# A decoder trunk's feed-forward pairs: both products of a weight chunk in a row for each operand, the third product's additions pinned ahead of weight conversions, and the down projection's first two tiles ending with their last term

## The chip, the cores and the metric

The kernel runs on one core of one Trainium2 chip. The metric is the device time of one execution in microseconds (us). Before the change it is 1483.27 us, the median of 3 runs (1482.81 to 1483.72). Lower is better.

## The reference

The program is a two-layer decoder trunk on 512 tokens of width 1024, in f32. Each layer adds a gated mixture of three token mixers and then a SwiGLU feed-forward network; the change touches only the second half of a layer:

```python
x = x + g1 * (merged @ w_out)
h2 = rmsnorm(x, norm2_w) * (1 + sc2) + sh2
x = x + g2 * ((jax.nn.silu(h2 @ w_gate) * (h2 @ w_up)) @ w_down)   # D_FF = 2816
```

## The kernel before, in words

**Data.** Activations lie transposed, 8 tiles of 128 features by 512 tokens (`x`, `norm`). Every f32 operand of a product is split into a high and a low part (`hi` by ScalarE, line 325 for weights and 510 for activations; `lo` by VectorE as the difference, lines 328 and 511). A product of two blocks is then three matmuls, hi by hi, hi by lo and lo by hi, issued by `mm3`, whose line 149 is the line of all of them. Weights stream from memory in chunks of 8 blocks of 128 by 128 into `raw` (3 buffers, loads on the SyncE queue, line 232). `split_w` turns a chunk into `whi` and `wlo` (4 buffers each). `next_w(ahead)` hands out the next chunk and starts the ones that follow, `ahead_now` = 3 unless an argument says otherwise.

**The feed-forward network.** The 22 columns of 128 hidden features are done in four parts, `PARTS` = ((3,1,1), (0,0,3), (0,0,2), (0,0,3)): so many columns along with the norm, so many single ones, so many pairs; then the down projection of the part's 6, 6, 4 and 6 columns is added to `x` (8 tiles, a residual on VectorE, line 954, for each). A layer has 9 pairs, the program 18.

**A pair** (`glu_pair`) computes gate and up of two columns for 512 tokens with 7 products in place of 8, on halves of 256 tokens. Operand z = 0 is gate, z = 1 is up. There are 14 groups of 12 matmuls of 256 columns: for each z the groups B21 (into a `pair` bank, e), B11 (into a), R1 (into c), -V (onto a), B22 (onto c), T3 (onto a) and T4 (onto a). Between groups that add onto the same bank the bank's value is read out: a after B11 (ScalarE copy, line 1063, and e added by VectorE, 1064), c after R1 (ScalarE, 1069), a after -V (ScalarE, 1072), c after B22 (VectorE addition, 1077) and a after T3 (VectorE addition, 1081). A group that adds onto a bank has to wait for the read-out before it. Before the change the groups stand in the order B21 z0, B21 z1, B11 z0, B11 z1, R1 z0, R1 z1, -V z0, -V z1, B22 z0, B22 z1, T3 z0, T3 z1, T4 z0, T4 z1.

A pair takes 7 chunks, called sub 0 to sub 6 here: subs 0 and 1 (gate and up, for B21 and B11), 2 and 3 (R1 and -V), 4 and 5 (B22 and T3), 6 (T4 of both). Subs 2 to 5 are sums of weight blocks that DMA accumulation (GpSimd queue, lines 254 and 256) and two VectorE additions (262, 263) make; those additions and the conversion of subs 0 and 1 of the next pair fall into the later part of this pair.

**What orders the work.** TensorE runs in program order. On the other engines a scheduler places instructions, but what goes through `pin` keeps its program order among the pinned ones; all weight conversions of line 328, the additions 262 and 263 and the modulation dot products (line 374, with 512 KB loads into 2 `dot` buffers, line 398) are pinned. The additions 1064, 1077 and 1081 were not. Each engine then executes its list strictly in order, so an instruction that waits holds all behind it.

**Down projection.** Tile n (of 8) takes blocks n*nk to n*nk+nk-1, with one term k for each hidden column of the part, k = 0 to nk-1 in order; the last two terms come from the last pair. Their split parts (lines 510 and 511) are made while TensorE ends the pair and begins the projection. In layer 0 the `bulk` list holds 16 dot products for layer 1's modulation, which are worked off beside the down projections of the first two parts.

Of the kernel before, what the change touches and what calls it, by code (L numbers as in the profile page):

```python
# [16 lines left out]
AF = mybir.ActivationFunctionType  # L17
# [8 lines left out]
KT = D // P  # L26
# [51 lines left out]
def hybrid_trunk(ctx, tc, xT, ws, ada, cols, pool_w, qk_w, crow, pos, con, out):  # L78
# [159 lines left out]
    class Sums:  # L238
        def __init__(self, l, m, j):
            self.l, self.m, self.j = l, m, j  # L240
# [474 lines left out]
    for l in range(L):  # L715
# [241 lines left out]
        def tail(src_of, wblk_of, part, nk, nrm, last, lead=None, halved=2):  # L957

            for n in range(KT - halved):
                if n == KT - halved - 1:  # L960
                    flush_bulk()
                o = ps_mm()
                for k in range(nk):
                    mm3(o, wblk_of(n, k), src_of(k), k == 0, k == nk - 1)
                residual(n, o, 0, S, part)
                if nrm is not None:
                    nrm.add(n, 0, S)
                if last:
                    nc.sync.dma_start(out[n * P:(n + 1) * P, :], x[n])
            for h in range(2):  # L970
                c = slice(h * BLOCK, (h + 1) * BLOCK)
                for n in range(KT - halved, KT):
                    o = ps_mm()
                    for k in range(nk):
                        mm3(o[:, :BLOCK], wblk_of(n, k), cut(src_of(k), slice(None), c), k == 0, k == nk - 1)
                    residual(n, o[:, :BLOCK], h * BLOCK, (h + 1) * BLOCK, part)
                    if nrm is not None:
                        nrm.add(n, h * BLOCK, (h + 1) * BLOCK)
                        if h == 1 and n == KT - halved:
                            lead()  # L980
                    if last:
                        nc.sync.dma_start(out[n * P:(n + 1) * P, c], x[n][:, c])

        class Blocks:
            def __init__(self, per, few=2):
                self.per, self.few, self.w = per, few, {}
# [63 lines left out]
        def glu_pair():  # L1050

            both = range(2)
            e = [ps_pair()[:, 0, :BLOCK] for _ in both]
            a, c = [None] * 2, [None] * 2
            one, two = [None] * 2, [None] * 2
            w = [next_w() for _ in both]
            for z in both:
                group(e[z], w[z], 1, "B21", True)
            for z in both:
                a[z], one[z] = ps_mm()[:, :BLOCK], tmp()  # L1060
                group(a[z], w[z], 0, "B11", True)
                C11 = one[z][:, :BLOCK]
                A.activation(C11, a[z], AF.Copy)
                V.tensor_add(C11, C11, e[z])
            w = [next_w() for _ in both]
            for z in both:
                c[z], two[z] = ps_mm()[:, :BLOCK], tmp()
                group(c[z], w[z], 0, "R1", True)
                A.activation(two[z][:, BLOCK:], c[z], AF.Copy)
            for z in both:  # L1070
                group(a[z], w[z], 1, "-V", False)
                A.activation(one[z][:, BLOCK:], a[z], AF.Copy)
            w = [next_w() for _ in both]
            for z in both:
                group(c[z], w[z], 0, "B22", False)
                C12 = one[z][:, BLOCK:]
                V.tensor_add(C12, C12, c[z])  # L1077
            for z in both:
                group(a[z], w[z], 1, "T3", False)
                m22 = two[z][:, BLOCK:]  # L1080
                V.tensor_add(m22, m22, a[z])  # L1081
            w = next_w()
            for z in both:
                group(a[z], w, z, "T4", False)

            (g1, u1), (g2, u2) = one, two
            A.activation(g1, g1, AF.Silu)
            A.activation(g2[:, BLOCK:], g2[:, BLOCK:], AF.Silu, scale=-1.0)
            A.activation(g2[:, :BLOCK], a[0], AF.Silu, scale=-1.0)
            V.tensor_mul(u1, u1, g1)  # L1090
            act.append(split_from(u1))
            V.scalar_tensor_tensor(u2[:, BLOCK:], u2[:, BLOCK:], -1.0, g2[:, BLOCK:], op0=ALU.mult, op1=ALU.mult)
            V.scalar_tensor_tensor(u2[:, :BLOCK], a[1], -1.0, g2[:, :BLOCK], op0=ALU.mult, op1=ALU.mult)
            act.append(split_from(u2))

        for part, (along, single, pairs) in enumerate(PARTS):
# [28 lines left out]
            if part == 0 and l + 1 < L:  # L1125
                bulk.extend(ada_tasks(l + 1, (SC1, SH1)))
            bulk_rate[0] = 1.5
            blk = Blocks(nk, 4)
            if part + 1 < len(PARTS):
                for n in range(KT):  # L1130
                    if n == KT // 2:
                        bulk_rate[0] = 0.0
                    o = ps_mm()
                    for k in range(nk):
                        mm3(o, blk(n, k), act[k], k == 0, k == nk - 1)
                    residual(n, o, 0, S, G2)
            elif l + 1 == L:
                tail(lambda k: act[k], blk, G2, nk, None, True)
            else:
                flush_bulk()  # L1140
                drain()
                n1 = Norm()
                table(AF.Abs_reciprocal_sqrt, f32(act[-1][1])[:, 0:1])
                scratch = ps_pair()
                bank = scratch[:, 1]
                tail(lambda k: act[k], blk, G2, nk, n1, False, lead(n1, l + 1, 0, bank), 4)
                norm = n1


# [98 lines left out]
```

## Time and profile before

| | before |
|---|---|
| median of 3 runs (range) | 1483.27 us (1482.81 to 1483.72) |
| profiled execution, span from first to last instruction | 1484.8 us |
| TensorE busy | 1460.9 us, 98% |
| VectorE busy | 1050.8 us, 71% |
| ScalarE busy | 662.0 us, 45% |
| GpSimd busy | 106.9 us, 7% |
| mean granted TensorE clock | 0.999 |
| from memory | 213.65 MB read, 145 GB/s over the span |

The profiled execution has no other time of its own than its span, which is 1.5 us above the median of the timed runs. A busy matmul in this profile is counted from its start to its modelled end, and ends overlap the next starts, so a stall is read best from the distance between the starts of two matmuls: back to back they start 0.12 us apart with 256 columns and 0.227 us apart with 512 columns.

### The profile page before, as it was taken

How to read it: one execution, taken by the hardware profiler on the slowest of the kernel's cores; microseconds unless marked ns; L12 is line 12 of the kernel's file. 1: busy time of each engine (PE TensorE's matmuls, PEld its weight loads, DVE VectorE, ACT ScalarE, POOL GpSimd, SP SyncE). 2: the span in 40 equal slices, each digit the busy share in tenths (PEclk: the TensorE clock that was granted, in tenths of full speed). 3: DMA queues.
4: the chain of work that ended last, by engine and by line, in shares of the span. 5: the costliest groups of instructions: out<-in, count | busy, mean ns of one | idle time of the engine just before them, and what ended most of it. 6: DMA issues, size and time to landing. Idle time of an engine off the chain costs nothing. (4 is left out here: it accounts for less than half of the span.)

```text
span 1484.8 us, 21967 instructions
## 1 busy us (share of the span) xinstructions
PE 1460.9 (98%) x8443; PEld 1269.0 (85%) x8443; DVE 1050.8 (71%) x1855; ACT 662.0 (45%) x1138; POOL 106.9 (7%) x157
## 2 busy tenths in 40 slices
PE   9999999999999999999999999999999999999999
PEld 7888787888988998989988877778889889989997
DVE  7877888758786866657576877776587756657673
ACT  4634555443553452535444345555335524434350
POOL 0000000020000220210000000001000102211100
PEclk9999999999999999999999999999999999999999
DMA  9624344475247675734323443334552445736432
GB/s 351 206 75 169 127 142 131 139 199 175 84 131 219 196 185 189 185 100 128 107 93 125 167 162 119 110 114 138 135 185 77 127 134 146 188 97 182 135 95 84
DMA packets 84408, 217.18 MB, mean 146 GB/s; under 512 B 10832, under 2 KB 23760, under 8 KB 84304
## 3 DMA queue, kind: packets, MB, share of 16 engines
q1 hardware_dynamic: 67456, 177.37, 35.5%
q0 software_dynamic: 16128, 37.76, 11.4%
q8 instruction: 66, 1.08, 0.3%
q10 hardware_dynamic: 720, 0.66, 0.1%
q14 instruction: 38, 0.31, 0.1%
HBM read 213.65 MB, written 2.10 MB: 145 GB/s over the span
## 5 line engine op out<-in xcount | busy, mean ns | idle before, releaser
L149 PE MATMUL mm<-big,whi 128*128 128x512 f32 (+1 forms) x4362 | 1086.1, 340 | 10.3 <-DVE tmp L1081 5.9
L149 PEld LDWEIGHTS mm<-big,whi 128*128 128x128 f32 x4362 | 746.3, 190 | 101.9 <-DVE tmp L1081 9.5
L149 PE MATMUL mm<-big,wlo 128*128 128x512 f32 (+1 forms) x2181 | 737.7, 338 | 0.3 <-DVE wlo L328 0.3
L149 PEld LDWEIGHTS mm<-big,wlo 128*128 128x128 f32 x2181 | 414.4, 190 | 45.4 <-DVE wlo L328 0.8
L325 ACT ACTIVATE whi<-raw 128x1024 fp32r<-128x1024 f32 (+2 forms) x240 | 248.7, 1037 | 323.2 <-PE mm L149 277.4
L328 DVE TENSOR_TENSOR wlo<-raw,whi 128x1024 fp32r<-128x1024 f32 (+2 forms) x240 | 285.5, 1195 | 94.8 <-ACT whi L325 94.2
L325 ACT ACTIVATE whi<-w 128x1024 fp32r<-128x1024 f32 x72 | 76.4, 1061 | 131.9 <-PE mm L149 75.8
L254 POOL DMA_DIRECT2D w<-in_ws x72 | 47.0, 681 | 1007.5 <-DVE wlo L328 732.4
L954 DVE SCALAR_TENSOR_TENSOR x<-mm,mod,x 128x512 f32<-128x512 f32 (+1 forms) x90 | 62.0, 690 | 78.7 <-PE mm L149 78.7
L374 DVE SCALAR_TENSOR_TENSOR dot<-dot,csil 128x1024 f32<-128x1024 f32 x80 | 97.2, 1222 | 22.9 <-DMA dot<-in_ada 22.6
L328 DVE TENSOR_TENSOR wlo<-w,whi 128x1024 fp32r<-128x1024 f32 x72 | 87.4, 1221 | 36.5 <-ACT whi L325 36.5
L149 PE MATMUL pair<-whi,big 128*128 128x512 f32 x224 | 76.8, 390 | 0.0
L256 POOL DMA_DIRECT2D w<-in_ws x72 | 64.1, 945 | 143.7 <-DMA w<-in_ws 132.6
L149 PE MATMUL pair<-big,whi 128*128 128x256 f32 (+1 forms) x376 | 74.1, 295 | 0.0
L149 PEld LDWEIGHTS pair<-big,whi 128*128 128x128 f32 x376 | 60.5, 191 | 2.2
L149 PE MATMUL mm<-whi,big 128*128 128x512 f32 x160 | 57.2, 394 | 1.5 <-ACT big L497 1.2
L149 PE MATMUL pair<-big,wlo 128*128 128x256 f32 (+1 forms) x188 | 55.5, 295 | 1.1 <-DVE wlo L328 1.1
L511 DVE TENSOR_TENSOR big<-tmp,big 128x512 fp32r<-128x512 f32 x48 | 32.9, 692 | 29.9 <-ACT big L510 28.9
L914 DVE SCALAR_TENSOR_TENSOR big<-big,mm 128x512 f32<-128x512 f32 x48 | 32.8, 685 | 23.8 <-PE mm L149 23.4
L149 PEld LDWEIGHTS pair<-whi,big 128*128 128x128 f32 x224 | 42.1, 188 | 8.7
L149 PE MATMUL pair<-wlo,big 128*128 128x512 f32 x112 | 43.7, 390 | 0.0
L630 ACT ACTIVATE w<-mm 128x512 fp32r<-128x512 f32 (+2 forms) x48 | 24.0, 525 | 33.4 <-PE mm L155 33.2
(187 smaller groups left out, 1249.8 us busy)
## 6 DMA issues: line engine op xcount, KB each, us to landing
raw<-in_ws SPq DMA_DIRECT2D x146, 512.0 KB, 3.3
dot<-in_ada SPq DMA_DIRECT2D x80, 512.0 KB, 4.1
w<-in_ws POOLq DMA_DIRECT2D x144, 256.0 KB, 4.4
raw<-in_ws SPq DMA_DIRECT2D x64, 256.0 KB, 3.7
raw<-in_ws SPq DMA_DIRECT2D x24, 384.0 KB, 3.3
w<-in_ada SPq DMA_DIRECT2D x16, 512.0 KB, 5.7
raw<-in_ws SPq DMA_DIRECT2D x16, 448.0 KB, 4.9
raw<-in_ws SPq DMA_DIRECT2D x36, 128.0 KB, 3.2
```

The source lines that it names most:

```text
L149: tc.keep_in_program_order(T.matmul(*a, **k))
L254: nc.gpsimd.dma_start(dst, self.source(0, 1))
L256: nc.gpsimd.dma_start(dst, self.source(*other), accum_op=ALU.add)
L325: A.activation(hi[:, :n], raw[:, :n], AF.Copy)
L328: ins = V.tensor_sub(lo[:, :n], raw[:, :n], f32(hi)[:, :n])
L374: return V.scalar_tensor_tensor(aw, aw, 1.0, csil, op0=ALU.mult, op1=ALU.mult, accum_out=mod[l][:, part, j:j + 1])
L511: V.tensor_sub(lo, src, f32(hi))
L630: A.activation(both[:, :, :, 0], tp, AF.Copy)
L914: V.scalar_tensor_tensor(sg, sg, 1.0, branch, op0=ALU.add, op1=ALU.mult)
L954: V.scalar_tensor_tensor(x[k][:, lo:hi], src, mod[l][:, part, k:k + 1], x[k][:, lo:hi], op0=ALU.mult, op1=ALU.add)
```

## The change

In `glu_pair` both products of a chunk follow each other for one operand, so the groups now stand in the order B21 z0, B11 z0, B21 z1, B11 z1, R1 z0, -V z0, R1 z1, -V z1, B22 z0, T3 z0, B22 z1, T3 z1, T4 z0, T4 z1, and each chunk is asked for just ahead of its own products. The three VectorE additions (now lines 1081, 1094 and 1096) are pinned. SiLU and product of the first column (now lines 1099 and 1100) stand ahead of the T4 groups in program order. In every down projection of the feed-forward network, tiles 0 and 1 are opened together (`open_tiles`, `late` = 1): all terms but the last of tile 0, all but the last of tile 1, then the last of each; chunks first used by these two tiles are asked for with `next_w(2)` rather than 3. The number of instructions on each engine is the same as before.

```diff
+        def open_tiles(src_of, wblk_of, nk, late):
+            os = [ps_mm(), ps_mm()]
+            for ks in (range(nk - late), range(nk - late, nk)):
+                for n, o in enumerate(os):
+                    for k in ks:
+                        mm3(o, wblk_of(n, k), src_of(k), k == 0, k == nk - 1)
+            return os
+
+        def whole_tiles(src_of, wblk_of, nk, late, count):
+            ready = open_tiles(src_of, wblk_of, nk, late) if late else []
+            for n in range(count):
+                if n < len(ready):
+                    o = ready[n]
+                else:
+                    o = ps_mm()
+                    for k in range(nk):
+                        mm3(o, wblk_of(n, k), src_of(k), k == 0, k == nk - 1)
+                yield n, o
...
-                    self.w[c] = next_w(2 if n >= KT - self.few else None)
+                    self.w[c] = next_w(2 if n >= KT - self.few or n < self.early else None)
...
-            e = [ps_pair()[:, 0, :BLOCK] for _ in both]
-            a, c = [None] * 2, [None] * 2
-            one, two = [None] * 2, [None] * 2
-            w = [next_w() for _ in both]
-            for z in both:
-                group(e[z], w[z], 1, "B21", True)
+            a, c, one, two = [], [], [], []
             for z in both:
-                a[z], one[z] = ps_mm()[:, :BLOCK], tmp()
-                group(a[z], w[z], 0, "B11", True)
+                w = next_w()
+                e = ps_pair()[:, 0, :BLOCK]
+                group(e, w, 1, "B21", True)
+                a.append(ps_mm()[:, :BLOCK])
+                group(a[z], w, 0, "B11", True)
+                one.append(tmp())
                 C11 = one[z][:, :BLOCK]
                 A.activation(C11, a[z], AF.Copy)
-                V.tensor_add(C11, C11, e[z])
-            w = [next_w() for _ in both]
+                pin(V.tensor_add(C11, C11, e))
...
-            w = [next_w() for _ in both]
-            for z in both:
-                group(c[z], w[z], 0, "B22", False)
-                C12 = one[z][:, BLOCK:]
-                V.tensor_add(C12, C12, c[z])
-            for z in both:
-                group(a[z], w[z], 1, "T3", False)
-                m22 = two[z][:, BLOCK:]
-                V.tensor_add(m22, m22, a[z])
+            for z in both:
+                w = next_w()
+                group(c[z], w, 0, "B22", False)
+                C12, C22 = one[z][:, BLOCK:], two[z][:, BLOCK:]
+                pin(V.tensor_add(C12, C12, c[z]))
+                group(a[z], w, 1, "T3", False)
+                pin(V.tensor_add(C22, C22, a[z]))
             w = next_w()
+            (g1, u1), (g2, u2) = one, two
+            A.activation(g1, g1, AF.Silu)
+            V.tensor_mul(u1, u1, g1)
+            act.append(split_from(u1))
...
-            blk = Blocks(nk, 4)
+            blk = Blocks(nk, 4, 2)
...
-                tail(lambda k: act[k], blk, G2, nk, None, True)
+                tail(lambda k: act[k], blk, G2, nk, None, True, late=1)
```

Three places show what moved. The first is VectorE's list in the second half of the first pair of layer 1's second part: `w4` are the weight sums, `wlo` the converted chunks, and `mm` is bank a or c. Before:

```order
L262 TENSOR_TENSOR w42151_11788<-w42151_11788,raw2172_11931 128x512
L263 TENSOR_TENSOR w42152_11789<-w42151_11788,raw2172_11931 128x512
L328 TENSOR_TENSOR wlo2174_11937<-raw2172_11931,whi2173_11935 128x1024
L262 TENSOR_TENSOR w42153_11794<-w42153_11794,raw2175_11939 128x512
L1077 TENSOR_TENSOR tmp2160_11833<-tmp2160_11833,mm2168_11875 128x256
L263 TENSOR_TENSOR w42154_11795<-w42153_11794,raw2175_11939 128x512
L1077 TENSOR_TENSOR tmp2162_11849<-tmp2162_11849,mm2170_11890 128x256
L1081 TENSOR_TENSOR tmp2169_11876<-tmp2169_11876,mm2159_11832 128x256
L1090 TENSOR_TENSOR tmp2162_11849<-tmp2162_11849,tmp2160_11833 128x512
L328 TENSOR_TENSOR wlo2177_11945<-raw2175_11939,whi2176_11943 128x1024
L1081 TENSOR_TENSOR tmp2171_11891<-tmp2171_11891,mm2161_11848 128x256
L328 TENSOR_TENSOR wlo2179_12001<-w42151_11788,whi2178_11999 128x1024
```

And now, at the same place, where 1094 is the addition after B22, 1096 the one after T3 and 1100 the product that was line 1090:

```order
L262 TENSOR_TENSOR w42149_11786<-w42149_11786,raw2172_11931 128x512
L263 TENSOR_TENSOR w42150_11787<-w42149_11786,raw2172_11931 128x512
L328 TENSOR_TENSOR wlo2174_11937<-raw2172_11931,whi2173_11935 128x1024
L1094 TENSOR_TENSOR tmp2157_11828<-tmp2157_11828,mm2165_11868 128x256
L1096 TENSOR_TENSOR tmp2166_11869<-tmp2166_11869,mm2156_11815 128x256
L262 TENSOR_TENSOR w42151_11792<-w42151_11792,raw2175_11965 128x512
L263 TENSOR_TENSOR w42152_11793<-w42151_11792,raw2175_11965 128x512
L328 TENSOR_TENSOR wlo2177_11971<-raw2175_11965,whi2176_11969 128x1024
L1094 TENSOR_TENSOR tmp2162_11861<-tmp2162_11861,mm2170_11903 128x256
L1096 TENSOR_TENSOR tmp2171_11904<-tmp2171_11904,mm2161_11848 128x256
L1100 TENSOR_TENSOR tmp2162_11861<-tmp2162_11861,tmp2157_11828 128x512
L328 TENSOR_TENSOR wlo2179_12001<-w42149_11786,whi2178_11999 128x1024
```

The second addition after T3 has moved from behind both the product (1090) and the conversion of sub 1 to ahead of the product; the conversion of sub 1 stands ahead of it in both lists.

The second place is VectorE's list at layer 0's first down projection, whose `dot` rows are the modulation products. Before, from the conversion of the projection's chunk 3 on (the chunks count from 0):

```order
L328 TENSOR_TENSOR wlo881_4448<-raw879_4441,whi880_4446 128x1024
L374 SCALAR_TENSOR_TENSOR dot882_4456,mod1_118<-dot882_4456,csil_89 128x1024
L374 SCALAR_TENSOR_TENSOR dot883_4459,mod1_118<-dot883_4459,csil_89 128x1024
L954 SCALAR_TENSOR_TENSOR x0_77<-mm878_4440,mod0_117,x0_77 128x512
L328 TENSOR_TENSOR wlo890_4496<-raw888_4491,whi889_4494 128x1024
L954 SCALAR_TENSOR_TENSOR x1_78<-mm887_4484,mod0_117,x1_78 128x512
L374 SCALAR_TENSOR_TENSOR dot884_4462,mod1_118<-dot884_4462,csil_89 128x1024
L374 SCALAR_TENSOR_TENSOR dot885_4465,mod1_118<-dot885_4465,csil_89 128x1024
```

And now, after two products (of `dot880` and `dot881`) and a third (`dot882`) that stand ahead of these rows:

```order
L954 SCALAR_TENSOR_TENSOR x0_77<-mm878_4440,mod0_117,x0_77 128x512
L374 SCALAR_TENSOR_TENSOR dot883_4457,mod1_118<-dot883_4457,csil_89 128x1024
L954 SCALAR_TENSOR_TENSOR x1_78<-mm879_4441,mod0_117,x1_78 128x512
L374 SCALAR_TENSOR_TENSOR dot884_4472,mod1_118<-dot884_4472,csil_89 128x1024
L328 TENSOR_TENSOR wlo887_4485<-raw885_4478,whi886_4483 128x1024
L374 SCALAR_TENSOR_TENSOR dot888_4496,mod1_118<-dot888_4496,csil_89 128x1024
L954 SCALAR_TENSOR_TENSOR x2_79<-mm889_4507,mod0_117,x2_79 128x512
L374 SCALAR_TENSOR_TENSOR dot890_4514,mod1_118<-dot890_4514,csil_89 128x1024
L954 SCALAR_TENSOR_TENSOR x3_80<-mm899_4553,mod0_117,x3_80 128x512
L374 SCALAR_TENSOR_TENSOR dot891_4517,mod1_118<-dot891_4517,csil_89 128x1024
L328 TENSOR_TENSOR wlo894_4531<-raw892_4526,whi893_4529 128x1024
L328 TENSOR_TENSOR wlo897_4539<-raw895_4533,whi896_4537 128x1024
```

The conversion of chunk 3 (`wlo887`) has moved from ahead of all dot products to behind five of them, that of chunk 4 (`wlo894`) from behind two to behind eight; on the SyncE queue five dot loads now stand ahead of the load of the next pair's sub 0.

The third place is TensorE's list where tile 0 of a down projection (`mm2255`) reaches its last two terms, in layer 1's second part. `big2251` and `big2253` are the last pair's two activations before the change, `big2180` is the first term's. Before:

```order
L149 MATMUL mm2255_12558<-big2251_12548,wlo2240_12436 128x512
L149 MATMUL mm2255_12558<-big2253_12554,whi2239_12434 128x512
L149 MATMUL mm2255_12558<-big2254_12555,whi2239_12434 128x512
L149 MATMUL mm2255_12558<-big2253_12554,wlo2240_12436 128x512
L149 MATMUL mm2259_12586<-big2180_12031,whi2239_12434 128x512
```

And now, where tile 1 is `mm2256` and five terms of it (15 matmuls) stand between the first row and the last four, of which the end is shown:

```order
L149 MATMUL mm2256_12559<-big2251_12522,wlo2243_12470 128x512
L149 MATMUL mm2255_12558<-big2253_12554,whi2239_12434 128x512
L149 MATMUL mm2255_12558<-big2254_12555,whi2239_12434 128x512
L149 MATMUL mm2255_12558<-big2253_12554,wlo2240_12436 128x512
L149 MATMUL mm2256_12559<-big2253_12554,whi2242_12468 128x512
```

The last term of tile 0 has moved behind the five other terms of tile 1.

More of the change, by code (lines that the diff above doesn't have):

```diff
@@ L955, in residual, with tail @@
                                    op0=ALU.mult, op1=ALU.add)
-        def tail(src_of, wblk_of, part, nk, nrm, last, lead=None, halved=2):
-            for n in range(KT - halved):
+        def open_tiles(src_of, wblk_of, nk, late):
[15 more added lines that the diff above has]
+                yield n, o
+        def tail(src_of, wblk_of, part, nk, nrm, last, lead=None, halved=2, late=0):
+            for n, o in whole_tiles(src_of, wblk_of, nk, late, KT - halved):
                 if n == KT - halved - 1:
                     flush_bulk()
-                o = ps_mm()
-                for k in range(nk):
-                    mm3(o, wblk_of(n, k), src_of(k), k == 0, k == nk - 1)
                 residual(n, o, 0, S, part)
@@ L984, in hybrid_trunk, with __init__ @@
         class Blocks:
-            def __init__(self, per, few=2):
-                self.per, self.few, self.w = per, few, {}
+            def __init__(self, per, few=2, early=0):
+                self.per, self.few, self.early, self.w = per, few, early, {}
             def __call__(self, n, k):
@@ L1062, in glu_pair @@
                 C11 = one[z][:, :BLOCK]
                 A.activation(C11, a[z], AF.Copy)
-                V.tensor_add(C11, C11, e[z])
-            w = [next_w() for _ in both]
+                pin(V.tensor_add(C11, C11, e))
             for z in both:
-                c[z], two[z] = ps_mm()[:, :BLOCK], tmp()
-                group(c[z], w[z], 0, "R1", True)
+                w = next_w()
+                c.append(ps_mm()[:, :BLOCK])
+                two.append(tmp())
+                group(c[z], w, 0, "R1", True)
@@ L1069, in glu_pair @@
                 A.activation(two[z][:, BLOCK:], c[z], AF.Copy)
+                group(a[z], w, 1, "-V", False)
+                A.activation(one[z][:, BLOCK:], a[z], AF.Copy)
             for z in both:
-                group(a[z], w[z], 1, "-V", False)
-                A.activation(one[z][:, BLOCK:], a[z], AF.Copy)
-            w = [next_w() for _ in both]
-            for z in both:
-                group(c[z], w[z], 0, "B22", False)
-                C12 = one[z][:, BLOCK:]
-                V.tensor_add(C12, C12, c[z])
@@ L1083, in glu_pair @@
+            (g1, u1), (g2, u2) = one, two
+            A.activation(g1, g1, AF.Silu)
+            V.tensor_mul(u1, u1, g1)
+            act.append(split_from(u1))
+            A.activation(g2[:, BLOCK:], g2[:, BLOCK:], AF.Silu, scale=-1.0)
+            V.scalar_tensor_tensor(u2[:, BLOCK:], u2[:, BLOCK:], -1.0, g2[:, BLOCK:], op0=ALU.mult, op1=ALU.mult)
             for z in both:
                 group(a[z], w, z, "T4", False)
-            (g1, u1), (g2, u2) = one, two
-            A.activation(g1, g1, AF.Silu)
@@ L1127, in hybrid_trunk @@
             bulk_rate[0] = 1.5
-            blk = Blocks(nk, 4)
+            blk = Blocks(nk, 4, 2)
             if part + 1 < len(PARTS):
-                for n in range(KT):
-                    if n == KT // 2:
+                for n, o in whole_tiles(lambda k: act[k], blk, nk, 1, KT):
+                    if n == KT // 2 - 1:
                         bulk_rate[0] = 0.0
-                    o = ps_mm()
-                    for k in range(nk):
-                        mm3(o, blk(n, k), act[k], k == 0, k == nk - 1)
                     residual(n, o, 0, S, G2)
             elif l + 1 == L:
-                tail(lambda k: act[k], blk, G2, nk, None, True)
+                tail(lambda k: act[k], blk, G2, nk, None, True, late=1)
             else:
```

7 lines of the change are left out of this document (2 added, 5 removed).

## The prediction

> **What bounds the kernel now.** I read the page's first part, then who waited for whom on TensorE's weight loads, then the timeline at those waits. The page says that TensorE is the bound:
>
> ```profile
> span 1484.8 us, 21967 instructions
> PE 1460.9 (98%) x8443; PEld 1269.0 (85%) x8443; DVE 1050.8 (71%) x1855; ACT 662.0 (45%) x1138; POOL 106.9 (7%) x157
> ```
>
> So only TensorE's own waits can be won; work taken off VectorE by itself is worth nothing. The waits of its weight loads name the ones that the change touches (total us, times, longest):
>
> ```profile
> PEld mm L149 <- DVE tmp L1081: 9.5, 18, 0.6
> PEld mm L149 <- DVE big L511: 2.5, 6, 0.5
> PEld mm L149 <- ACT big L510: 2.1, 2, 1.7
> PEld pair L149 <- DVE wlo L328: 1.3, 1, 1.3
> ```
>
> There are 18 pairs, and the first row has 18 waits: one in each pair, for the addition after T3. The next two wait for the last pair's activation, the fourth for a converted weight chunk ahead of a pair. The timeline of TensorE in the first pair of layer 1's second part (start, duration, idle time before and its releaser) shows which group waits:
>
> ```profile
> 1227.07 0.40 PE L149 MATMUL pair<-big,whi 128*128 128x256 f32 x2
> ...
> 1245.67 0.28 PE L149 MATMUL mm<-big,wlo 128*128 128x256 f32 x1
> 1246.33 0.50 PE L149 MATMUL mm<-big,whi 128*128 128x256 f32 x2 [0.38 <-DVE tmp L1081]
> ...
> 1247.86 0.40 PE L149 MATMUL pair<-big,whi 128*128 128x256 f32 x2
> ```
>
> A pair is 14 groups of 12 matmuls of 0.12 us, 1.44 us a group and 20.16 us in all, but 1247.86 - 1227.07 = 20.79 us pass. The row at 1246.33 stands 12 matmuls ahead of the pair's end, so T4 of z = 1 waits, not T4 of z = 0. It should have started at 1245.79, lost 0.54, and its first two matmuls take 0.50 together where two take 0.40 in the row at 1247.86: 0.64 us in all. VectorE in the same stretch says why:
>
> ```profile
> 1242.86 0.69 DVE L263 TENSOR_TENSOR w<-w,raw 128x512 f32<-128x512 f32 x1
> 1243.46 0.42 DVE L1077 TENSOR_TENSOR tmp<-tmp,mm 128x256 f32<-128x256 f32 x1
> 1243.79 0.42 DVE L1081 TENSOR_TENSOR tmp<-tmp,mm 128x256 f32<-128x256 f32 x1
> 1244.12 0.69 DVE L1090 TENSOR_TENSOR tmp<-tmp,tmp 128x512 f32<-128x512 f32 x1
> 1244.72 1.22 DVE L328 TENSOR_TENSOR wlo<-raw,whi 128x1024 fp32r<-128x1024 f32 x1
> 1245.86 0.42 DVE L1081 TENSOR_TENSOR tmp<-tmp,mm 128x256 f32<-128x256 f32 x1
> ```
>
> T3 of z = 1 ended at 1227.07 + 12 x 1.44 = 1244.35; its addition came at 1245.86, behind a product (1090) and a conversion. VectorE has no idle time in these rows: it is late, not waiting. In the last pair of a part the loss is smaller:
>
> ```profile
> 1268.66 0.40 PE L149 MATMUL pair<-big,whi 128*128 128x256 f32 x2
> ...
> 1289.35 0.40 PE L149 MATMUL mm<-big,whi 128*128 128x512 f32 x1
> ```
>
> 1289.35 - 1268.66 = 20.69, 0.53 us over 20.16.
>
> **The change part by part: the pairs.** 10 pairs have another behind them, 8 are the last of a part: 10 x 0.64 + 8 x 0.53 = 10.6 us to win, if T4 of z = 1 no longer waits. The group row bounds it from above: 9.5 us of idle weight loads and 18 x 0.10 of restart, 11.3. What is late next? I lay the new order on the same clock, with the pair's start as zero. Lags and ScalarE's conversion are in these rows:
>
> ```profile
> 1234.46 0.38 ACT L1069 ACTIVATE tmp<-mm 128x256 f32<-128x256 f32 x1 [0.23 <-PE mm L149]
> 1237.22 1.06 ACT L325 ACTIVATE whi<-raw 128x1024 fp32r<-128x1024 f32 x1 [0.94 <-PE mm L149]
> ```
>
> R1 of z = 0 ended at 7.20 (1234.27), and its reader started 0.19 later; -V of z = 0 ended at 10.08 (1237.15), and the conversion that its weight buffer released started 0.07 later. In the new order T3 of z = 0 ends at 14.40, so its addition starts at 14.59 at the earliest. Behind it VectorE has 262 and 263, the conversion of sub 1, the addition after B22 and the one after T3 of z = 1. By the distances of the quoted rows that is 0.33 + 2 x 0.60 + 1.14 + 0.33, so the last addition starts at 17.59 (T3 of z = 1 is ready at 17.28 + 0.19) and ends at 18.01. T4 of z = 1 is due at 13 x 1.44 = 18.72: 0.7 us to spare. The conversion needs its high part: the buffer is free at 14.47, a SiLU shorter than a conversion stands ahead, so it is done by 14.47 + 2 x 1.06 = 16.6 at the latest where VectorE arrives at 16.1; that takes at most 0.5 of the 0.7. T4 of z = 0 gains a group of distance and had not waited. The other read-outs keep three groups (4.3 us) between write and next use. Weight buffers get freer: a chunk is used for two groups in a row, not over five. The pinned additions now wait ahead of conversions: behind them stands sub 1's, ready at about 17.3 and needed at 20.16 + 2.88 = 23.0. GpSimd's list has one accumulation begun earlier; SyncE's order within pairs is as before. I take 10.5 us.
>
> **The down projections.** In layer 0's third part ScalarE and TensorE show the wait for the last activation, and the windows the granted clock behind it (column PEclk, 0.50 and 0.65):
>
> ```profile
> 630.87 1.06 ACT L325 ACTIVATE whi<-raw 128x1024 fp32r<-128x1024 f32 x1 [2.68 <-DMA raw<-in_ws]
> 631.84 0.61 ACT L510 ACTIVATE big<-tmp 128x512 fp32r<-128x512 f32 x1
> 630.79 0.39 PE L149 MATMUL mm<-big,wlo 128*128 128x512 f32 x1
> 632.50 0.51 PE L149 MATMUL mm<-big,whi 128*128 128x512 f32 x1 [1.32 <-ACT big L510]
> 633.23 0.51 PE L149 MATMUL mm<-big,whi 128*128 128x512 f32 x1 [0.22 <-DVE big L511]
> 634.00:636.00 2.00, 2.00 (x6) 1.54 (x5) 0.97 (x2) 0.00 (x0) 0.00 (x0) 0.50 0.25 84
> 636.00:638.00 2.00, 2.00 (x7) 1.56 (x7) 0.00 (x0) 0.00 (x0) 0.00 (x0) 0.65 0.48 178
> ```
>
> The split of the last activation stood behind a chunk's conversion that waited for its load. TensorE lost 632.50 - 630.79 - 0.227 = 1.48 and 633.23 - 632.50 - 0.227 = 0.50, 1.98 us, where the weight loads' waits count 1.7 + 0.5 = 2.2, so a matmul loses 0.9 of what its weight load waits. Of the group rows' 2.5 + 2.1 = 4.6 us I expect 0.8 to 0.9: 3.7. The last term of tile 0 now comes nk - 1 terms later, each 3 x 0.227 = 0.68: 2.0 us later with nk = 4, 3.4 with nk = 6. That covers every one of these waits but, just, the largest: its high part came 1.48 late, its low part 633.23 - 632.50 later still, and the start comes half a us earlier. I leave 0.3 (0 to 1.0 over the two parts with four columns).
>
> The half clock cost (2 x 0.50 + 2 x 0.35) = 1.7 us. The timed runs have a median 1.5 us below the profile's span, so they may not have it; I count half, 0.9. [...]
>
> **The dot products in layer 0.** This is where the change may cost. Rows of VectorE and TensorE at the first down projection and behind it:
>
> ```profile
> 458.05 0.63 PE L149 MATMUL mm<-big,whi 128*128 128x512 f32 x2
> 460.92 0.69 DVE L511 TENSOR_TENSOR big<-tmp,big 128x512 fp32r<-128x512 f32 x1 [2.17 <-ACT big L510]
> 468.36 1.23 DVE L374 SCALAR_TENSOR_TENSOR dot<-dot,csil 128x1024 f32<-128x1024 f32 x1 [0.86 <-DMA dot<-in_ada]
> 474.12 1.22 DVE L374 SCALAR_TENSOR_TENSOR dot<-dot,csil 128x1024 f32<-128x1024 f32 x1 [1.94 <-DMA dot<-in_ada]
> 475.82 1.23 DVE L374 SCALAR_TENSOR_TENSOR dot<-dot,csil 128x1024 f32<-128x1024 f32 x1 [0.47 <-DMA dot<-in_ada]
> 478.63 1.23 DVE L374 SCALAR_TENSOR_TENSOR dot<-dot,csil 128x1024 f32<-128x1024 f32 x1 [0.92 <-DMA dot<-in_ada]
> 481.39 1.23 DVE L374 SCALAR_TENSOR_TENSOR dot<-dot,csil 128x1024 f32<-128x1024 f32 x1 [1.52 <-DMA dot<-in_ada]
> 493.79 0.39 PE L149 MATMUL pair<-big,wlo 128*128 128x256 f32 x1 [1.14 <-DVE wlo L328]
> dot<-in_ada SPq DMA_DIRECT2D x80, 512.0 KB, 4.1
> ```
>
> With two buffers a dot product follows the one two before it by a load and a product: 474.12 - 468.36 = 5.76, 478.63 - 474.12 = 4.51 and 481.39 - 475.82 = 5.57 us, mean 5.28. Chunk 4's conversion now stands behind eight products, two loaded long before. The first starts 3.5 us after the projection's start D (460.92 + 0.6 against 458.05), the second 1.15 later, the eighth three turns after the second: 4.65 + 3 x 5.28 = 20.5; product and conversion add 2.3: ready at D + 22.8. Chunk 4 starts with block 32 and its low part is used 0.45 later: 32 x 0.68 + 0.45 = D + 22.2. So TensorE waits 0.6 us (0 at turns of 4.5, 2.1 at 5.8). Chunk 3, behind five products, is ready at 4.65 + 5.28 + 2.3 + 1.2 = 13.4 plus residuals, due at 16.8. The second part has fewer products ahead: no wait. [...]
>
> The wait at 493.79 goes: it lost 1.3 and 0.1 since sub 1 was needed one group into the pair and now two. 1.4 won; if the queue of dots runs late instead, 0.
>
> **Sum.** 10.5 + 3.7 + 0.9 + 1.4 - 0.3 - 0.6 = 15.6 us. From the median 1483.27 that is 1467.7 us; the span would go from 1484.8 to 1469.2, or 1468.4 with all of the half clock gone.
>
> **The rivals.** (a) The dot queue costs more: turns of 5.8 us, 2.1 us of wait, and behind it another 3.4 us at half clock, 1.7; with 493.79 not won: 1467.7 + 1.5 + 1.7 + 1.4 = 1472.3. For it: the idle times before the products, all by DMA. Against: the two next-pair loads now come later. (b) The additions are in order, but VectorE arrives over 0.7 us late and T4 waits as before, because 262 waits for accumulations: 1467.7 + 10.5 = 1478.2. Against: VectorE has no idle time before 263 in the rows. (c) The change doesn't do what it says: every wait goes over to the next releaser; 1483. Against: the 0.7 us worked out. (d) Slower: the pinned additions hold conversions. If the sums of sub 1 land so late that 262 starts 2.3 us behind its place, 0.7 to spare and then 1.6 us a pair, the ten pairs with another behind lose 16 us, as much as the sum above gains; at 3.0 us late in each it is 1467.7 + 10 x (3.0 - 0.7) = 1490.7. Against: the same rows, and that the accumulations are begun no later.
>
> **How the numbers follow.** Forecast 0.76, (a) 0.12, (b) 0.06, (c) 0.03, (d) 0.03. The range's lower end: 11.3 + 4.6 + 1.7 + 1.4 = 19 us at the very most, of which I allow 18.3: 1465.0. The upper end holds (a) with its unknowns, 1473.5. It leaves out (b), (c) and (d), 0.12, and some of the edges. About 0.2% (3 us) is what a measurement can tell from no change: faster in the forecast, (a) and (b), 0.94; same (c), 0.03; slower (d), 0.03.
>
> **What would show it.** Right: no wait of T4 on line 1096, pairs of 20.16 us, no wait for lines 510 or 511 at a projection's start, at most one wait of 0 to 2 us for a conversion near 22 us into layer 0's first projection. Wrong: 18 waits that only name another line, VectorE idle ahead of 262, or half-clock windows in layer 0.

## The result and the profile after

The kernel after takes 1470.59 us (median of 4 runs, 1469.69 to 1471.74), the kernel before 1483.49 (4 runs, 1482.81 to 1484.62): ratio 0.9914, interval 0.9900 to 0.9928, so 12.9 us won. The forecast was 1467.7 with a range of 1465.0 to 1473.5: the sign and the range held, the gain was 2.7 us too large. Two executions of the study, one of the kernel before (5098 us) and one of e7 (2386 us), took far longer than all others and are in none of the medians below.

The page's first part, beside the one of before:

```profile
span 1467.9 us, 21907 instructions
PE 1452.6 (99%) x8443; PEld 1266.3 (86%) x8443; DVE 1050.9 (72%) x1855; ACT 664.4 (45%) x1138; POOL 106.9 (7%) x157
```

VectorE does as much as before, and TensorE is busy 8.3 us less: matmuls that restart behind a wait or run at half clock are counted longer (0.50 and 0.63 us against 0.40 in rows below). The waits of TensorE's weight loads for lines 328 and 511 that are left (total us, times, longest; of the first row only the longest, 0.7, lies in the feed-forward network):

```profile
PEld mm L149 <- DVE wlo L328: 1.0, 3, 0.7
PEld mm L149 <- DVE big L511: 0.3, 1, 0.3
```

The row with 18 waits for the addition after T3 is gone, and no other took its place: line 1096 stands in no row. The timeline of TensorE in the first pair of layer 1's second part, the same pair as in the prediction:

```profile
1215.56 0.40 PE L149 MATMUL pair<-big,whi 128*128 128x256 f32 x2
...
1234.27 0.40 PE L149 MATMUL mm<-big,whi 128*128 128x256 f32 x2
...
1235.71 0.28 PE L149 MATMUL pair<-big,whi 128*128 128x256 f32 x1
```

1235.71 - 1215.56 is 20.15 us, 14 groups at full pace, and T4 of z = 1 starts at 18.71 into the pair without a wait. VectorE in that pair:

```profile
1232.95 0.42 DVE L1094 TENSOR_TENSOR tmp<-tmp,mm 128x256 f32<-128x256 f32 x1
1233.29 0.41 DVE L1096 TENSOR_TENSOR tmp<-tmp,mm 128x256 f32<-128x256 f32 x1
1233.62 0.69 DVE L1100 TENSOR_TENSOR tmp<-tmp,tmp 128x512 f32<-128x512 f32 x1
1234.22 1.22 DVE L328 TENSOR_TENSOR wlo<-w,whi 128x1024 fp32r<-128x1024 f32 x1
```

The last addition starts 17.73 us into the pair and ends at 18.14 (forecast 17.59 and 18.01), with product and conversion behind it. 0.58 us are to spare, where 0.7 were forecast.

One wait is left in layer 0's first down projection, at the place that the prediction names:

```profile
479.82 0.50 PE L149 MATMUL mm<-big,wlo 128*128 128x512 f32 x1 [0.23 <-DVE wlo L328]
```

By the starts it lost 0.39 us and 0.11 at the next matmul, 0.5 against 0.6 forecast. Over the whole program the distances between TensorE's starts exceed full pace by some 17 us more in the profile of before than here; in the feed-forward parts alone they exceed it by 17.4 us there and 0.7 here. So the traces say 17 us and the clock says 12.9. That difference is what the first experiment is about.

### The profile page after: what moved, and what is told of

The parts are those of the page before. It is cut to its first block, busy times and chain, and to the rows that moved or that the text cites. A ratio compares the mean times of both kernels' runs of the same rounds, so it can differ in the third digit from the quotient of the medians.

```text
span 1467.9 us, 21907 instructions
## 1 busy us (share of the span) xinstructions
PE 1452.6 (99%) x8443; PEld 1266.3 (86%) x8443; DVE 1050.9 (72%) x1855; ACT 664.4 (45%) x1138; POOL 106.9 (7%) x157
## 3 DMA queue, kind: packets, MB, share of 16 engines
q0 software_dynamic: 16128, 37.76, 11.9%
## 4 chain that ended last, share of the span: by engine, by line
PE 88%; DVE 7%; DMA 2%; ACT 2%; issue 1%; SPq 0%; DVEq 0%; ACTq 0%
PE mm L149 75%; PE pair L149 11%; PE mm L155 2%; DMA dot<-in_ada 2%; DVE wlo L328 1%; DVE dot L374 1%; ACT whi L325 1%; DMA w<-in_ada 0%; ACT tmp L612 0%; ACT tmp L614 0%; DMA x<-in_xT 0%; DVE tmp L619 0%; DVE w L374 0%; DVE big L514 0%; DVE big L914 0%
## 5 line engine op out<-in xcount | busy, mean ns | idle before, releaser
L1081 DVE TENSOR_TENSOR tmp<-tmp,pair 128x256 f32<-128x256 f32 x36 | 15.2, 422 | 40.1 <-ACT tmp L1080 40.1
```

The costliest lines, as they stand in the source:

```text
L1081: pin(V.tensor_add(C11, C11, e))
```

## The experiments

**e1: the kernel before, once more.** No edit.

> The kernel before, unchanged, to see how much of its profiled execution's stalls belong to every execution. Theory A (my sum, as it stands): the wait of 1.98 us around 632.50 and the 1.7 us at half clock behind it are in about half of all executions; the new profile's span is 1483 to 1485 us, and a stretch with PEclk about 0.5 may be there. Theory B (the one profile was a slow one): time minus span is 1.8 us in the kernel after, so timed runs of 1483.3 us have spans of about 1481.6, 3 us under the profile's 1484.8; the new profile shows about 1481.6, no half clock between 634 and 638 us, and a wait under 0.5 us at the third part's down projection. The 18 waits of T4 (10.6 us with their restarts) stand in both.

Measured: 1483.68 us (11 runs), 1483.06 for its comparison runs (21), ratio 1.0006 (0.9997 to 1.0015). The profiled execution has a span of 1480.7 us, 4.1 less than the first profile. Its waits:

```profile
PEld mm L149 <- DVE tmp L1081: 9.6, 18, 0.6
PEld mm L149 <- DVE big L511: 1.4, 4, 0.5
PEld mm L149 <- DVE wlo L328: 0.9, 1, 0.9
PEld mm L149 <- ACT big L510: 0.5, 2, 0.3
```

And TensorE at the third part's down projection, where the first profile had lost 1.98 us and then 1.6 at half clock:

```profile
630.25 0.49 PE L149 MATMUL mm<-big,whi 128*128 128x512 f32 x1
630.97 0.50 PE L149 MATMUL mm<-big,whi 128*128 128x512 f32 x1 [0.23 <-DVE big L511]
631.32 0.40 PE L149 MATMUL mm<-big,wlo 128*128 128x512 f32 x1
```

Here 0.6 are lost and the clock stays up. The wait for a chunk ahead of a pair (1.4 at 493.79) isn't there either; the 0.9 for line 328 lies outside the feed-forward network. The 18 waits of T4 are the same to 0.1 us. Theory B holds: the pairs' loss belongs to every execution, the others differ from one to the next. They end with a load. ScalarE's conversion ahead of the last split, whose row of the first profile (630.87) the prediction shows, waits for its load here too, but less:

```profile
628.62 1.06 ACT L325 ACTIVATE whi<-raw 128x1024 fp32r<-128x1024 f32 x1 [1.85 <-DMA raw<-in_ws]
```

Counted from the late start of T4 in the pair before it (626.61 here, 627.41 there) it starts 2.0 us on and not 3.5. At 493.79 it is the load of a dot product: that product waited 0.78 us for it at 487.11 in the first profile, and not at all here. In the runs that list both, the time is the span plus 1.8 us. The first profile's execution therefore took about 1486.6 us, as long as the longest of the 61 timed runs of this kernel in the study (1480.9 to 1486.5, median 1483.1).

**e2 and e3: the two halves of the change.** e2 has the new `glu_pair` and the down projections as before; against the kernel after it is

```diff
-            blk = Blocks(nk, 4, 2)
+            blk = Blocks(nk, 4)
...
-                for n, o in whole_tiles(lambda k: act[k], blk, nk, 1, KT):
+                for n in range(KT):
...
+                    o = ps_mm()
+                    for k in range(nk):
+                        mm3(o, blk(n, k), act[k], k == 0, k == nk - 1)
```

e3 has the down projections of after and the `glu_pair` of before, without pins; its diff against after is that of the function in the section on the change, the other way round.

> Only the new order of the pairs (with its pins); the down projections open their tiles one after the other as before. My sum: 10.5 us for 18 waits of T4 and 1.4 for the wait at 493.79, so 1483.5 - 11.9 = 1471.6 us, and the waits for lines 510 and 511 at the projections' starts (3.6 us of TensorE in before) still there in the profile. Rival (the profile overstated the pairs too, by the ratio of the measured 12.9 us to the 15.6 predicted): 1483.5 - 9.8 = 1473.7. Rival (the pairs' wins come only together with the down edit): under 8 us won.

> Only the down projections' new start (late 1, early 2); the pairs as before. My sum: 3.7 - 0.3 - 0.6 = 2.8 us, and 0.9 of half clock, so 1480.7 down to 1479.8 us, and the 18 waits of T4 still there. Theory B (the big wait and the half clock are seldom in a timed run): 3.7 less 1.98 less 0.6 of dot products is 1.1 us won, 1482.4. Rival (the dot products ahead of chunk 4 eat it): 1483.5 or slower.

Measured: e2 1473.20 us (5 runs), ratio 0.9939 (0.9927 to 0.9951), 9.9 us won where I expected 11.9. e3 1481.19 (11 runs), ratio 0.9988 (0.9980 to 0.9997), 1.9 won, between the sum and theory B. Together 11.8, between the 12.9 that the whole change won here and the 10.9 that it won beside e11 below: within what such comparisons differ by, the halves add up. They are not independent, though, as e2's waits show:

```profile
PEld mm L149 <- DVE big L511: 3.4, 6, 0.8
PEld mm L149 <- ACT big L510: 3.1, 3, 1.0
```

6.5 us of waits at the projections' starts, against 1.9 in e1 and 4.6 in the first profile of before: pairs that no longer wait reach the projection before the last activation is split. The stalls of T4 had been hiding a part of the starts' wait. In e2's profiled execution (its slowest, 1476.75 us) the half clock came as well:

```profile
628.27 0.50 PE L149 MATMUL mm<-big,whi 128*128 128x512 f32 x1 [0.42 <-DVE big L511]
...
629.60 0.50 PE L149 MATMUL mm<-big,whi 128*128 128x512 f32 x1 [0.60 <-ACT big L510]
630.33 0.63 PE L149 MATMUL mm<-big,whi 128*128 128x512 f32 x1 [0.22 <-DVE big L511]
630.76 0.63 PE L149 MATMUL mm<-big,wlo 128*128 128x512 f32 x1
```

Three gaps of 0.58, 0.77 and 0.50 us, none as long as the 1.48 of the first profile of before, and from 630.33 on matmuls start 0.427 us apart instead of 0.227.

**e4: only the pins,** in before's order of groups:

```diff
-                V.tensor_add(C11, C11, e[z])
+                pin(V.tensor_add(C11, C11, e[z]))
-                V.tensor_add(C12, C12, c[z])
+                pin(V.tensor_add(C12, C12, c[z]))
-                V.tensor_add(m22, m22, a[z])
+                pin(V.tensor_add(m22, m22, a[z]))
```

> Before's order of groups, with its three additions pinned and nothing else: VectorE then does both additions after T3 ahead of the product and of one conversion. My theory (the group order makes the room): T3 of z = 0 ends at 15.84 us into the pair and T4 of z = 0 is due at 17.28, 1.44 later, and a conversion of 1.2 us and the additions after B22 stand ahead of its addition, so T4 waits still, now for z = 0 as well: 0 to 4 us won, 1480 to 1483.5. Rival (the pins do all of it, the group order nothing): all 18 waits go, 10.5 us won, 1473.0. Rival (pins hold conversions): slower than before by 2 us or more, with waits for converted chunks in the pairs.

Measured: 1521.92 us (5 runs), ratio 1.0252 (1.0236 to 1.0268), 38.9 us slower. Neither my 0 to 4 won nor the rival's 10.5: T4 now waits much longer, and for z = 0.

```profile
PEld mm L149 <- DVE tmp L1081: 36.9, 18, 2.1
```

ScalarE, VectorE and TensorE in one pair:

```profile
1262.99 1.06 ACT L325 ACTIVATE whi<-raw 128x1024 fp32r<-128x1024 f32 x1 [2.99 <-PE mm L149]
1264.08 1.22 DVE L328 TENSOR_TENSOR wlo<-raw,whi 128x1024 fp32r<-128x1024 f32 x1 [0.74 <-ACT whi L325]
1265.22 0.74 DVE L1077 TENSOR_TENSOR tmp<-tmp,mm 128x256 f32<-128x256 f32 x2
1265.88 0.75 DVE L1081 TENSOR_TENSOR tmp<-tmp,mm 128x256 f32<-128x256 f32 x2
1266.35 0.51 PE L149 MATMUL mm<-big,whi 128*128 128x256 f32 x2 [1.84 <-DVE tmp L1081]
```

All four additions run together, in order, and all late: a conversion now stands ahead of them whose high part waits for a buffer, and that buffer comes free when T3 of z = 0 ends. T4 of z = 0 was due at 1264.35 and starts at 1266.35. The rival that pins hold conversions had the sign, with the parts exchanged: a conversion holds the additions. In the change itself the pins do nothing: the program built without them, and with SiLU and product behind T4 again, has its instructions in the same order on all five engines, row for row; it was not run. So the order of the groups, with the requests for chunks that go with it, is all there is to the pairs' gain.

**e9 and e10: which groups.** e9 changes only the third row (B22, T3, B22, T3) of before's `glu_pair`, e10 only the first two, in the same way for B21 with B11 and for R1 with -V; neither has pins. e9 against before:

```diff
-            w = [next_w() for _ in both]
             for z in both:
-                group(c[z], w[z], 0, "B22", False)
+                w = next_w()
+                group(c[z], w, 0, "B22", False)
...
-            for z in both:
-                group(a[z], w[z], 1, "T3", False)
+                group(a[z], w, 1, "T3", False)
```

> The kernel before with one thing of the change: B22 z0, T3 z0, B22 z1, T3 z1 in that order, each chunk asked for ahead of its own two groups; no pins, the first eight groups and the down projections as before. In the ten pairs with another behind them VectorE then has, behind the addition after B22 of z = 1, one 263 and one conversion ahead of the last addition. My theory (only the place of the last addition matters): it starts 15.84 + 0.19 + 0.33 + 0.60 + 1.14 = 18.1 us into the pair and ends at 18.5, T4 of z = 1 is due at 18.72, so nothing waits, with 0.2 to spare: as the pairs-only kernel, 1473 us. Rival (the conversion's high part comes late, since its buffer is free only when T3 of z = 0 ends): up to 0.5 us in each of ten pairs, 1473 to 1478. Rival (the first eight groups' order is needed too): the 18 waits stay, 1483.

> The other part of the pairs' change alone: B21 z0, B11 z0, B21 z1, B11 z1, R1 z0, -V z0, R1 z1, -V z1, each chunk asked for ahead of its own groups; B22, T3 and everything else as before, no pins. My theory: the last addition still stands behind a product and a conversion, so the 18 waits on the addition after T3 stay: 1483 us, within 1.5. Rival (buffers that come free sooner let VectorE run ahead, and that was the gain): 1473 us.

Measured on one chip: e9 1476.04 us (6 runs), ratio 0.9952 (0.9937 to 0.9967); e10 1475.61 (5 runs), ratio 0.9953 (0.9941 to 0.9965). e9 went as expected in the pairs: no wait for an addition is left, although the last one has only some 0.1 us to spare. In the pair that began at 1220.14 it ends 18.60 us in:

```profile
1238.33 0.41 DVE L1080 TENSOR_TENSOR tmp<-tmp,mm 128x256 f32<-128x256 f32 x1
```

Its time is 3 us over the 1473 that I expected, and its six runs lie far apart (1472.5 to 1479.3). What it lacks stands at the starts, 4.4 us of waits for line 511 and 4.1 for 510. e10 went against my theory, which gave it nothing:

```profile
PEld mm L149 <- DVE tmp L1079: 3.8, 8, 0.5
```

8 of the 18 waits are left, those of the pairs that are the last of a part; the ten others are gone. A timeline of VectorE in one of the ten, which began at 1218.49:

```profile
1228.29 1.23 DVE L328 TENSOR_TENSOR wlo<-raw,whi 128x1024 fp32r<-128x1024 f32 x1 [1.05 <-ACT whi L325]
...
1234.37 0.69 DVE L1088 TENSOR_TENSOR tmp<-tmp,tmp 128x512 f32<-128x512 f32 x1
1234.98 0.41 DVE L1079 TENSOR_TENSOR tmp<-tmp,mm 128x256 f32<-128x256 f32 x1
1235.54 1.23 DVE L328 TENSOR_TENSOR wlo<-raw,whi 128x1024 fp32r<-128x1024 f32 x1 [0.15 <-ACT whi L325]
1236.68 0.41 DVE L1079 TENSOR_TENSOR tmp<-tmp,mm 128x256 f32<-128x256 f32 x1
```

The last addition is still behind a conversion, as I had said, but it ends at 18.60, not at 19.2: chunks used for two groups in a row free their buffers sooner. ScalarE's conversion ahead of the first row starts 8.71 us into the pair, just behind the end of -V of z = 0 at 8.64 (10.15 and 10.08 in the same pair of before). The conversion in the first row then starts at 9.80 (11.24 in before), and the last addition comes 0.6 us earlier. So either row alone is enough for the ten pairs, by two different ways, and the third row is needed for the eight.

**e5: how much is to spare, and when the clock drops.** Extra additions ahead of the last one, in another number for each pair:

```diff
+EXTRA = ((1, 1, 2, 3, 4, 6, 7, 8, 9), (2, 7, 8, 9, 10, 2, 12, 8, 3))
...
+                for _ in range(EXTRA[l][pairs_done[0]] if z else 0):
+                    pin(V.tensor_add(two[1][:, :BLOCK], one[1][:, :BLOCK], one[1][:, :BLOCK]))
                 pin(V.tensor_add(C22, C22, a[z]))
+            pairs_done[0] += 1
```

> The kernel after, with n extra additions of 256 columns on VectorE (0.33 us each) ahead of the addition after T3 of z = 1; n is 1, 1, 2, 3, 4, 6, 7, 8, 9 for the nine pairs of layer 0 and 2, 7, 8, 9, 10, 2, 12, 8, 3 for those of layer 1. The extra sums go to a buffer that is overwritten later; the output is the same. My theory: in the trace of after that addition ends 18.14 us into a pair and T4 of z = 1 is due at 18.72, so 0.58 us are to spare and T4 waits 0.33 n - 0.58: nothing for 1, 0.1 for 2, 0.4 for 3, 2.06 for 8, 3.4 for 12; over the ladder 24 us and 1.5 of restarts. Rival: that addition is not what is next in line (a conversion or a SiLU is), and the first step that costs is another. On the clock: theory G (a fixed grid of windows of 3.41 us, half clock for one window when more than about 1.9 us of the window before was idle) gives stretches of 3.4 us at half clock, 1.5 us lost in each, behind some of the gaps of 2.06 us and more and behind none of the shorter ones: about 1503 us in all. [...]

Measured: 1515.4 us (one run). T4 waits in 14 pairs, for that addition and nothing else:

```profile
PEld mm L150 <- DVE tmp L1101: 33.9, 14, 4.9
```

By the starts, the pairs with another behind them lose 0.28 us with 2 extras, 1.19 with 4, 2.58 with 7, 3.04 with 8, 3.95 with 10 and 4.88 with 12: 0.46 n - 0.64. An extra addition cost 0.46 (six take 2.72 us together), not the 0.33 that I took from additions into different buffers, which makes 9 of the 12 us by which the total is over my figure; two starts of projections behind late pairs lose 0.9 each. The line's foot, 0.64, agrees with the 0.58 of the trace and the 0.7 forecast. In the last pairs of a part 3, 6 and 9 extras lose 0.37, 1.75 and 3.13, on a line of 0.46 n - 1.01.

The clock went by theory G. In e4 ten of the 18 waits of 2.0 us are followed by half clock, and the ends of all ten stretches lie on one grid of 3.413 us, within 0.09. Windows of that grid in e4 (length, busy time of PE, PEld, DVE, ACT, POOL, then PEclk):

```profile
1264.44:1267.85 3.41, 1.57 (x13) 1.50 (x13) 3.41 (x7) 2.10 (x3) 0.00 (x0) 1.00 1.04 265
1267.85:1271.26 3.41, 3.41 (x18) 3.41 (x17) 1.97 (x4) 1.62 (x3) 0.57 (x1) 0.50 0.58 213
1308.82:1312.23 3.41, 1.69 (x15) 1.48 (x13) 2.15 (x5) 1.06 (x1) 0.00 (x0) 1.00 1.07 252
1312.23:1315.64 3.41, 3.29 (x26) 3.25 (x27) 2.56 (x5) 2.65 (x5) 0.00 (x0) 1.00 0.93 293
```

The first wait lies almost whole in one window, with its restart, and the next window runs at half clock; the second wait reaches over a border, and nothing follows. Counted by the starts, over all fourteen profiles from 420 us on and with the borders 0.06 us ahead of the changes of clock that the profile records, each of the 19 windows at full clock that lost 1.97 us or more has a window at half clock behind it, and none has that lost 1.94 or less. With the borders on the recorded changes the two sides overlap, 1.97 against 2.00, so they are told apart to some 0.05 us. In e5 a wait of 3.04 us that a border cut (1.92 and 1.12) cost nothing more, and another of 3.04, whole in one window, cost 1.4. A window at half clock in which TensorE still stood for 1.3 to 1.4 us (e5 from 1426.28, e8 from 486.63) was followed by another one.

**e6 and e12: the lookahead.** The kernel after, with three chunks asked for ahead at the first tiles, as before:

```diff
-            blk = Blocks(nk, 4, 2)
+            blk = Blocks(nk, 4)
```

> The kernel after, with the chunks of the first two tiles asked for three ahead again (early 0); late stays 1. Theory A (the later last term alone covers the starts): no wait for lines 510 or 511 at a projection's start, chunk 4's conversion stands behind five dot products and not eight, so the 0.5 us at 22 us into layer 0's first projection go: 1470.1 us. Rival (the lookahead of two is what keeps a conversion from standing ahead of the last split): waits of 0.3 to 2 us for 510 or 511 come back at one or more of the eight starts, 1471 to 1473 us.

> The kernel after without the shorter lookahead (early 0), a second time beside the kernel after: my theory gives 0.6 us less than it, 1470.0 us, and no wait in the feed-forward parts. Rival: the 1.1 us between their medians so far is more than that wait and the shorter lookahead costs something else as well, 1469.5 us.

**e11: the kernel after, beside e12 on the same chip.** No edit.

> The kernel after, unchanged, for the comparison with the next one: 1470.6 us; the profile has a wait of 0.5 us, with 0.1 of restart, for chunk 4's low part in layer 0's first down projection and no other over 0.3 in the feed-forward parts.

Measured: e6 1469.47 us (4 runs), ratio 0.9912 (0.9896 to 0.9928). On the other chip e12 1469.07 (4 runs, 1468.52 to 1469.41), ratio 0.9909 (0.9896 to 0.9922), and e11 1471.53 (5 runs, 1470.63 to 1473.29), ratio 0.9927 (0.9915 to 0.9939). The intervals against before overlap; the runs of e12 and e11 do not, 2.5 us lie between their medians, more than the 0.6 that I expected. (On this chip the kernel after is 10.9 us under the kernel before, 12.9 on the first.) e11's profile, of its run of 1473.29 us, says why:

```profile
PEld mm L149 <- DVE wlo L328: 2.5, 2, 2.3
PEld mm L149 <- DVE big L511: 1.4, 2, 1.2
```

```profile
481.47 0.50 PE L149 MATMUL mm<-big,wlo 128*128 128x512 f32 x1 [1.85 <-DVE wlo L328]
```

```profile
478.56:481.97 3.41, 1.56 (x7) 1.02 (x6) 2.93 (x4) 0.28 (x1) 0.00 (x0) 1.00 0.43 150
481.97:485.38 3.41, 3.41 (x9) 2.61 (x9) 3.41 (x7) 0.00 (x0) 0.00 (x0) 0.52 0.87 283
```

The wait for chunk 4's low part lost 2.0 us here, not 0.4, and a window at half clock behind it 1.5 more. VectorE's row of a dot product ahead of it, in this profile and in the first one of after:

```profile
470.63 1.23 DVE L374 SCALAR_TENSOR_TENSOR dot<-dot,csil 128x1024 f32<-128x1024 f32 x1 [1.99 <-DMA dot<-in_ada]
```

```profile
469.08 1.23 DVE L374 SCALAR_TENSOR_TENSOR dot<-dot,csil 128x1024 f32<-128x1024 f32 x1 [0.99 <-DMA dot<-in_ada]
```

VectorE's first dot product of the projection stood 0.5 us later in e11 (460.05 against 459.54), this load landed another us later, and the conversion three products on came 1.6 us later. In both profiles of the kernel with three chunks ahead this wait is gone; e12's has a start left (1.2 us of waits for line 511), as e11's has. The shorter lookahead thus buys nothing that these traces show and costs 0.5 to 3.7 us at one place. e6 and e12 are the fastest kernel of the study.

**e7: the late last term taken away,** with the short lookahead kept:

```diff
-                for n, o in whole_tiles(lambda k: act[k], blk, nk, 1, KT):
+                for n, o in whole_tiles(lambda k: act[k], blk, nk, 0, KT):
...
-                tail(lambda k: act[k], blk, G2, nk, None, True, late=1)
+                tail(lambda k: act[k], blk, G2, nk, None, True, late=0)
...
-                tail(lambda k: act[k], blk, G2, nk, n1, False, lead(n1, l + 1, 0, bank), 4, 1)
+                tail(lambda k: act[k], blk, G2, nk, n1, False, lead(n1, l + 1, 0, bank), 4, 0)
```

> The kernel after, with the first two tiles of a down projection summed one after the other (late 0); chunks are still asked for two ahead. Theory A (the later last term covers the starts): the waits of the pairs-only kernel come back, 5.3 us in the six starts that its profile shows, less what the shorter lookahead saves: 2 to 5 us lost, 1472.6 to 1475.6 us. Rival (the lookahead does it): under 1 us of such waits, 1470.6 to 1471.5.

Measured: 1474.20 us (4 runs, 1471.64 to 1475.50), ratio 0.9940 (0.9926 to 0.9954). Theory A holds: 5.6 us of waits at the starts are back.

```profile
PEld mm L149 <- DVE big L511: 3.5, 6, 1.0
PEld mm L149 <- ACT big L510: 2.1, 2, 1.0
```

**e8: dot products at twice the rate.**

```diff
-            bulk_rate[0] = 1.5
+            bulk_rate[0] = 3.0
             blk = Blocks(nk, 4, 2)
```

> The kernel after, with the dot products given out at twice the rate (3.0 for 1.5) in the down projections: chunk 4's conversion of layer 0's first projection then stands behind eleven and not eight. Theory A (VectorE serves the dot products at the pace of their loads, two in 5.28 us, and the conversion waits its turn): three more are 7.9 us, so TensorE waits 8.4 us there for line 328 instead of 0.5, and one window at half clock behind it, 1.5: 1480 us. Rival (the loads run together when asked for sooner, so that the products are through as early as before): 0 to 2 us, 1470.6 to 1472.6.

Measured: 1479.44 us (10 runs), ratio 0.9979 (0.9970 to 0.9988), 8.9 us slower than after in its first measurement; expected 1480. One wait carries it, 7.6 us by the starts against 8.4 expected:

```profile
487.94 0.79 PE L149 MATMUL mm<-big,wlo 128*128 128x512 f32 x1 [7.44 <-DVE wlo L328]
```

Behind it the clock is at half until 493.46, which loses 2.7 us more where 1.5 were expected for one window: three windows in a row have the half clock here. So the price of a turn, two products in 5.28 us, holds to 0.7 us: three products more in the queue cost 7.2 us here, expected were 7.9.

## Why the prediction was right, and where its size was off

The sum's terms, by its own steps:

| term | forecast | measured |
|---|---|---|
| pairs | 10.5 | 10.6: the 18 waits with their restarts, gone |
| starts of the down projections | 3.7, less 0.3 left | 3.6 in the first profile of before, 1.4 in e1's; 0.1 and 1.2 left in the two of after |
| half clock | 0.9 | 1.6 in the first profile, 0 in e1's |
| wait at 493.79 | 1.4 | 1.4 in the first profile, 0 in e1's; 0.7 in e9's |
| dot products | -0.6 | -0.5 in the first profile of after, -3.7 in e11's |

**The pairs** were right, in the mechanism and in the size: the last addition came 0.14 us behind the clock that I laid out, and the ladder found 0.64 us to spare. The reason that I gave was too narrow: T4 stops waiting by either of two ways (e9, e10). The pins, which I counted as part of the mechanism, are none of it.

**The step that failed** is the line "From the median 1483.27 that is 1467.7 us". I took what one profiled execution had lost off the median of others. For the half clock I asked whether the timed runs have it, and counted half; for the starts and for 493.79 I did not ask, though those waits end with a load's landing too. Time is span plus 1.8 us, so that execution was some 3 us over the median, and that is the error: in e1's profile the feed-forward network loses 12.0 us, not 17.4, of which 10.6 are the pairs. Against 12.0 the sum would have been 10.5 + 1.4 - 0.6 = 11.3 us, and 1472.0; measured were 12.9 and, in e11, 10.9. (e1's execution, 1482.4 us, was itself 0.7 us under the median of the 61, so an execution at the median loses somewhat more than 12.0.)

**Rival (a)** was not a rival but a part of the runs: its 2.1 us of wait with a window at half clock behind came in e11's profile as 2.0 and 1.5, and that run took 1473.29 us where the rival had 1472.3. For the wait on the dot products the forecast had 0.6 and the rival 2.1; the same kernel took 0.5 in one profile and 2.0 in the other. The rival's other part, that 493.79 is not won, did not come. (b) and (c) fell: no wait went over to another releaser. (d) did not come in the change, but e4 shows its mechanism with the parts exchanged, a conversion holding additions, at 2.0 us a pair.

**The clock.** The sum took the half clock, read from one profile, as a consequence of the two gaps ahead of it, 1.48 and 0.50 us. The runs agree: behind e2's three gaps (1.97 us by the starts, restarts counted) and behind ten of e4's single waits of 2.0 us the granted clock was a half for 3.41 us, and e4's ten stretches end on one grid of 3.413 us.

## What to carry to other kernels

Before taking a wait's time off a median, ask whether the wait ends with an engine's work, which the two profiles of before repeat to 0.1 us, or with a load, which came 1.0 to 1.5 us later in one profile here than in another of the same kernel; profile the kernel twice and compare the span with the timed runs. Where a wait at one stage's end goes, price the next stage's start again: it had been covered by that wait. Pinning an instruction puts it behind every pinned one ahead of it in the program, so look at what each is then queued behind, and whether that is waiting for TensorE itself; in e4 this cost 38.9 us.

## What the runs showed of the hardware

The half clock came in stretches of 3.41 us: PEclk was 0.50 from 633.98 us in the first profile of before and from 1267.85 in e4's, 0.52 from 481.97 in e11's. In the 3.41 us ahead of these TensorE had lost 2.1 us by the starts in before and 2.0 in e11, and 1.97 in e2 ahead of its stretch from 630.34; a window of e5 that had lost 1.92 (from 692.36) had full clock behind it. In the first profile of after PEclk was 1.00 from 420 to 1465 us. The stretch cost 1.6 us in before and 1.5 in e11, with TensorE busy throughout. So e11's wait cost 3.5 us with it; in e4 ten of the 18 waits of 2.0 us had a stretch at half clock behind them, and eight had not.
